# A hybrid FoX/S5 trunk: the mixer's phase doublings moved into pairs 4 to 8 of the first gate and up product, the transposes of c pinned behind their product group

## The chip, the core and the metric

The kernel runs on one core of a Trainium2 chip. The metric is the device time of one execution in microseconds (us), the median of several runs. Engines are named as in the profile: PE is the matrix engine (PEld its weight loads), DVE the vector engine, ACT the scalar engine, POOL the GpSimd engine, SP the engine that issues all DMAs here.

## The reference

Two layers over a sequence of 1024 tokens with 1024 features, all in float32. Layer 0 mixes tokens with forgetting attention, layer 1 with a diagonal complex state-space mixer (S5). Each mixer is followed by a SwiGLU channel mixer of 2816 hidden features, with norms around everything:

```python
for i in range(DEPTH):
    h = rmsnorm(x, mix_pre_gain[i])
    m = fox_mixer(h, ...) if i % 2 == 0 else s5_mixer(h, ...)
    x = x + rmsnorm(m, mix_post_gain[i])
    h = rmsnorm(x, ffn_pre_gain[i])
    x = x + rmsnorm((silu(h @ w_gate[i]) * (h @ w_up[i])) @ w_down[i], ffn_post_gain[i])
```

The S5 mixer needs tables that depend on parameters alone, not on x. From log_dt and lam it forms a = exp(lam dt) (with sine and cosine of the angle), z = (a - 1) / lam, and bb = z * b; it also uses c. These tables are what the change touches.

## The kernel before

The program is recorded in Python, and a list scheduler then places each instruction into its engine's stream by priority; each engine works its own stream strictly in order and waits on semaphores. `keep_in_program_order(op)` holds one instruction back to the place where the program wrote it; without it an instruction may be hoisted or sink. All DMAs stand in one stream, SP's.

**The product of gate and up** (`gate_up`, L830 to L987) works over 11 pairs p = 0 to 10 of 128-row blocks. A pair has 14 product groups s = 0 to 13, each of 12 matmuls (L882; three for each of four k, because every operand is kept as a high and a low part, `ah` and `al`, with `h*h + h*l + l*h`). It is a fast-matrix-product scheme: seven products per m = 0, 1, in the order `A11 B11`, `A12 B21`, `S1 T1`, `S2 T2`, `S3 T3`, `S4 B22`, `A22 T4`, so s = 2 i + m. The products land in PSUM banks X, Y and Z. After each group an eviction copies (ACT, L932, L937, L939) or adds (DVE, L934, L941, L944) the bank into the tiles `s` and `up`, and a bank is written again only when its eviction is done. DVE and ACT also split the next operands: ACT casts the high part (L851), DVE subtracts for the low part (L852), after sums of weight blocks (L864, L865, L870, L871). Weights come by DMA into four `raw` pages (L232), each freed by its last reader. The results go to DRAM (`g_d`, L959 to L967). All streams share PE with this chain of matmuls.

**The tables of the mixer** are a generator, `s5_params`, which `gate_up` advances one step at chosen (p, s) through `next(beside)`; which ones stands in `first` in `trunk`. Its steps, in order: dt and angles; exponentials; sines; powers of a (`powers(pw, 8)`); the phase doublings; z; then bb = z * b (`cmul`, L1211 to L1216) and the four loads of c (L1233); two steps of eight 128x128 PE transposes of c (L1239), each copied out by ACT into `cc` (L1243); then for eight chunks `ch` a chain of POOL products (L1269 to L1273, into `cp`), ACT copies of bb into a block `bs` (L1272), 16 small PE matmuls (L1287), POOL products again (L1330 to L1332, into `bp`), eight PE transposes (L1255), an ACT copy (L1257) and a store `T_d` (L1258). One chunk fills one pair, from pair 3 on. The next chunk's first POOL product writes the page that the store of `T_d` reads.

**The phase doublings** (L1182 to L1193 before) double a table X of angles four times: for n = 1, 2, 4, 8 the entries n+1 to 2n (7 of them at the end) are the first ones plus entry n, brought back into plus or minus pi by six DVE instructions (L1184 to L1189), each on the result of the last. X is read only much later, by `s5_rot` (L1311, after the gate and up product). Their scratch N is the tile `kk` on page 28, which `powers` uses before, and page 28 is also that of `bb`: bb can be written only when the last doubling has read N.

**Pages.** b is loaded on page 34, the scratch of bb's product is on page 32; the two halves of c are loaded into pages 34 and 32 again, so a load of c waits for the last product that reads b or that scratch. The page of R2 holds small tables in columns 512 and up and has its columns 0 to 447 free.

Of the kernel before, what the change touches and what calls it, by code (L numbers as in the profile page):

```python
# [12 lines left out]
ALU = mybir.AluOpType  # L13

P = 128
# [10 lines left out]
MAGIC = 1.5 * 2.0 ** 23  # L26
# [132 lines left out]
class Trunk:  # L159
# [668 lines left out]
    def gate_up(self, B, g_d, beside=iter(()), when=lambda p, s: False):  # L828
# [7 lines left out]
        nc, R = self.nc, self.R  # L836
        V = nc.vector
        n = NF // 2
# [64 lines left out]
        for p, s in order:  # L903
# [22 lines left out]
            m = s % 2  # L926
            a, b, x = steps[s // 2]
            mm(p, m, a, b, bank[x, m], s < 6)
            X, Y, Q = (bank[i, m] for i in "XYZ")
# [52 lines left out]
                prep[s - 10](1)  # L982
            if when(p, s):
                next(beside, None)
        yield

    def down(self, finish, begin=lambda tb, m: None, beside=iter(()), steps=((),) * 3, extra=0, last=3,  # L987
# [89 lines left out]
    def s5_small(self):  # L1077


        nc, A, c, R = self.nc, self.A, self.cst, self.R  # L1080
        V = nc.vector
        tt, ts, stt = V.tensor_tensor, V.tensor_scalar, V.scalar_tensor_tensor
# [17 lines left out]
        ps = self.pb((0, 1), (P, 4, 32))  # L1100
# [26 lines left out]
        ang, n, r = (w[:, 8 + 3 * i:11 + 3 * i] for i in range(3))  # L1127
# [4 lines left out]
        C1 = 6.28125  # L1132
        C2 = math.floor((2 * math.pi - C1) * 2 ** 20) / 2 ** 20
        C3 = 2 * math.pi - C1 - C2
        LIM = 3.141592
# [24 lines left out]
        X = self.ph.rearrange("p i a n -> p n (i a)")  # L1160
# [5 lines left out]
        kk = R("s5t2", (P, 2, 16, 32))  # L1166

        def powers(X, top):
            n = 1
            while n < top:  # L1170
                c_ = min(n, top - n)
                self.cmul(X[:, 0, n + 1:n + 1 + c_], X[:, 1, n + 1:n + 1 + c_], X[:, 0, 1:1 + c_], X[:, 1, 1:1 + c_],
                          X[:, 0, n:n + 1].to_broadcast([P, c_, 32]), X[:, 1, n:n + 1].to_broadcast([P, c_, 32]),
                          kk[:, 0, :c_], kk[:, 1, :c_])
                n += c_

        yield
        powers(pw, 8)
        yield
        n, N = 1, kk.rearrange("p i n a -> p (i n a)").rearrange("p (n m) -> p n m", m=64)  # L1180
        while n < 15:
            c_ = min(n, 15 - n)  # L1182
            x, q = X[:, n + 1:n + 1 + c_], N[:, :c_]
            tt(x, X[:, 1:1 + c_], X[:, n:n + 1].to_broadcast([P, c_, 64]), op=ALU.add)  # L1184
            ts(q, x, 1.0 / (2 * math.pi), MAGIC, op0=ALU.mult, op1=ALU.add)
            V.tensor_scalar_sub(q, q, MAGIC)
            stt(x, q, -C1, x, op0=ALU.mult, op1=ALU.add)
            stt(x, q, C1 - 2 * math.pi, x, op0=ALU.mult, op1=ALU.add)
            ts(x, x, LIM, -LIM, op0=ALU.min, op1=ALU.max)  # L1189
            n += c_  # L1190
            if n == 8:
                yield

        z = self.z = c.tile([P, 2, 32], F32, name="z5")
        u1, u2, u3, nre = tmp(), tmp(), tmp(), tmp()
        ar, ai = Pre[:, 1], Pim[:, 1]
# [21 lines left out]
    def s5_params(self):  # L1218


        nc, A, R = self.nc, self.A, self.R
# [3 lines left out]
        braw, kk = self.braw, R("s5w1", (P, 2, 32, 16))  # L1225
# [4 lines left out]
        craw = [R(f"s5w{i}", (P, 8, 2, HD)) for i in range(2)]  # L1230
# [4 lines left out]
        for i in range(2):  # L1235
            yield
            ps = self.S("psC", (P, 8, P))
            for t in range(8):
                nc.tensor.transpose(ps[:, t], craw[i][:, t].rearrange("p d s -> p (d s)"), self.ident)  # L1239

            for d in range(2):
                r = slice(d * 64, d * 64 + 64)
                nc.scalar.copy(self.cc[r, i].rearrange("p (t a) c -> p t a c", t=8),  # L1243
                               ps[r].rearrange("p t (a b c) -> p t a b c", b=2, c=16)[:, :, :, d])
# [347 lines left out]
def trunk(ctx: ExitStack, tc: tile.TileContext, A, out):  # L1592
    T = Trunk(ctx, tc, A, out)
    nc, R = T.nc, T.R
# [87 lines left out]
    T.fox(hT, og_d, first_norm(range(2, 8), (2, 3, -2, -1)), OUT0)  # L1682
    xr = x0.rearrange("(p b) d -> p b d", b=8)
    R.set(hold=[28, 30, 31, 34, 36, 37], t1=[20], ah=[3, 4, 20], al=[5, 6, 21], er=[29, 32])
    first = {0: (8, 10, 12), 1: (5, 6, 8, 10, 12), 2: (5, 8, 12)}
    B = Operands(T)
    gu = T.gate_up(B, g_d[0], T.s5_params(), lambda p, s: s in first.get(p, (5, 12)))
    end = T.out_proj(lambda tb: xr[:, tb, :], A["mix_post_gain"][0], A["ffn_pre_gain"][0], x1_d, turns, B, lambda: next(gu))
# [130 lines left out]
```

## Time and profile before

| | us |
|---|---|
| median of 3 runs | 2381.59 (2380.56 to 2382.78) |
| the profiled execution | 2379.95 |
| its span | 2378.1 |
| PE busy in the span | 2340.3 (98%) |
| DVE, ACT, POOL busy | 1683.0, 1195.2, 424.1 |

The span runs from the first to the last instruction; 1.85 us of the profiled execution lie outside it. A matmul shows as about 390 ns, but the next one starts some 227 ns behind it: they overlap, so distances are read from starts, not from busy time. In a timeline a row has the start, the duration, the engine, the line, the operation and its tiles, and in brackets the idle time of the engine before it and what ended that. The windows give busy time (and count) of PE, PEld, DVE, ACT and POOL, then the mean clock granted to PE (PEclk), the DMA share and GB/s. Pair 2 of the first gate and up product begins at 811.46 us, pair 4 at about 900, pair 9 at about 1101.

### The profile page before, as it was taken

The numbers are of one execution on the slowest core, as the hardware profiler recorded it, in microseconds if no ns is written. First come the engines' busy times: TensorE is split into PE (matmuls) and PEld (weight loads), VectorE is DVE, ScalarE is ACT, GpSimd is POOL, SyncE is SP. The second block draws the span as 40 slices with busy tenths as digits, with TensorE's granted clock in tenths as the row PEclk, the third lists the DMA queues.
The fourth block names the chain that finished last, engine by engine and source line by source line (L and its number), as shares of the span: only waits on it lengthen the run. The fifth ranks groups of instructions, "written<-read, shape, count | busy, mean of one in ns | idle before, by whom it ended". The sixth has DMA issues, their size and how long they took to land.

```text
span 2378.1 us, 31540 instructions
## 1 busy us (share of the span) xinstructions
PE 2340.3 (98%) x11736; PEld 1942.7 (82%) x11736; DVE 1683.0 (71%) x2684; ACT 1195.2 (50%) x2024; POOL 424.1 (18%) x411
## 2 busy tenths in 40 slices
PE   8999999999999999999999999999999999999998
PEld 6788888888788778888888889888888888888887
DVE  7867787678778966666778686853796656555867
ACT  6766676677745334444554662332463333333443
POOL 3222221222200034545520002410000000000000
PEclk9999999999999999999999999999999999999999
DMA  5121112211433444343598753443434323237874
GB/s 162 37 62 54 54 54 62 63 45 63 139 129 110 120 112 139 118 139 118 184 329 311 268 177 93 148 138 106 131 102 142 111 93 109 91 120 256 289 247 168
DMA packets 256684, 320.61 MB, mean 135 GB/s; under 512 B 34313, under 2 KB 184129, under 8 KB 256530
## 3 DMA queue, kind: packets, MB, share of 16 engines
q1 hardware_dynamic: 256530, 318.59, 41.3%
q8 instruction: 92, 1.51, 0.3%
q14 instruction: 62, 0.51, 0.1%
HBM read 240.82 MB, written 77.72 MB: 134 GB/s over the span
## 4 chain that ended last, share of the span: by engine, by line
PE 80%; DVE 10%; ACT 5%; issue 3%; POOL 1%; DMA 1%; DVEq 0%; SPq 0%; ACTq 0%; POOLq 0%
PE ps L882 32%; PE ps L1003 16%; PE ps L274 7%; PE ps L275 7%; PE ps L276 7%; PE ps L644 2%; PE ps L625 2%; PE ps L586 1%; DVE ps L590 1%; PE ps L587 1%; DVE y L329 1%; DVE ptl L629 1%; ACT y L298 1%; POOL o L652 1%; DMA raw<-in_ffn_w_gate_dram 1%
## 5 line engine op out<-in xcount | busy, mean ns | idle before, releaser
L882 PE MATMUL ps<-B,ah 128*128 128x512 f32 x992 | 306.5, 390 | 0.8 <-DVE B L90 0.6
L1003 PE MATMUL ps<-wdh,gh 128*128 128x512 f32 x616 | 240.0, 390 | 0.6 <-DVE s L924 0.6
L1003 PE MATMUL ps<-wdl,gh 128*128 128x512 f32 x616 | 239.9, 389 | 0.0
L1003 PE MATMUL ps<-wdh,gl 128*128 128x512 f32 x616 | 239.6, 389 | 0.1
L882 PE MATMUL ps<-ops,ah 128*128 128x512 f32 x704 | 220.0, 394 | 1.6 <-ACT s L939 1.6
L882 PEld LDWEIGHTS ps<-B,ah 128*128 128x128 f32 x992 | 186.2, 188 | 40.9 <-DVE B L90 1.2
L274 PE MATMUL ps<-hT,wh 128*128 128x512 f32 x496 | 197.4, 398 | 0.7 <-DVE pt L465 0.2
L276 PE MATMUL ps<-hT,wl 128*128 128x512 f32 x496 | 195.0, 393 | 0.0
L275 PE MATMUL ps<-hT,wh 128*128 128x512 f32 x496 | 194.5, 392 | 0.0
L882 PE MATMUL ps<-B,al 128*128 128x512 f32 x496 | 193.0, 389 | 0.0
L255 ACT CAST gh<-gr 128x1024 fp32r<-128x1024 f32 (+1 forms) x78 | 81.1, 1040 | 163.8 <-PE ps L1003 149.6
L882 PEld LDWEIGHTS ps<-ops,ah 128*128 128x128 f32 x704 | 132.4, 189 | 31.1 <-ACT s L939 2.1
L256 DVE TENSOR_TENSOR gl<-gr,gh 128x1024 fp32r<-128x1024 f32 (+1 forms) x78 | 98.8, 1268 | 79.5 <-ACT gh L255 79.1
L852 DVE TENSOR_TENSOR al<-raw,ah 128x1024 fp32r<-128x1024 f32 x84 | 109.1, 1301 | 55.5 <-ACT ah L851 55.3
L629 DVE TENSOR_TENSOR ptl<-ps,pth 128x512 fp32r<-128x512 f32 x192 | 102.5, 551 | 55.2 <-ACT pth L628 54.3
L1755 POOL TENSOR_TENSOR y<-m,s 128x512 f32<-128x512 f32 x4 | 6.5, 1645 | 750.3 <-DVE m L1030 652.8
L882 PE MATMUL ps<-ops,al 128*128 128x512 f32 x352 | 137.7, 391 | 0.0
L581 POOL TENSOR_TENSOR An<-An,cmask 128x128 f32<-128x128 f32 x128 | 75.4, 591 | 345.8 <-DVE mx L590 321.0
L1003 PEld LDWEIGHTS ps<-wdh,gh 128*128 128x128 f32 x616 | 115.6, 188 | 25.4 <-DVE s L924 1.3
L1003 PEld LDWEIGHTS ps<-wdh,gl 128*128 128x128 f32 x616 | 115.6, 188 | 24.5 <-DVE gl L256 0.5
L1003 PEld LDWEIGHTS ps<-wdl,gh 128*128 128x128 f32 x616 | 115.6, 188 | 23.6
L851 ACT CAST ah<-raw 128x1024 fp32r<-128x1024 f32 x84 | 88.3, 1052 | 90.6 <-PE ps L882 84.4
(393 smaller groups left out, 5886.6 us busy)
## 6 DMA issues: line engine op xcount, KB each, us to landing
raw<-in_ffn_w_down_dram SPq DMA_DIRECT2D x98, 512.0 KB, 5.3
gr<-g_d SPq DMA_DIRECT2D x76, 512.0 KB, 4.5
raw<-in_ffn_w_gate_dram SPq DMA_DIRECT2D x44, 512.0 KB, 4.0
raw<-in_ffn_w_up_dram SPq DMA_DIRECT2D x44, 512.0 KB, 4.5
g_d<-s SPq DMA_DIRECT2D x66, 256.0 KB, 2.0
raw<-in_fox_w_in_dram SPq DMA_DIRECT2D x32, 512.0 KB, 4.3
g_d<-up SPq DMA_DIRECT2D x44, 256.0 KB, 3.1
g_d<-up SPq DMA_DIRECT2D x21, 512.0 KB, 2.7
```

The costliest lines, as they stand in the source:

```text
L255: self.hop = self.hcopy(h, src)
L256: self.lop = self.lsub.tensor_sub(l, src, f32(h))
L274: mm(ps, lh, rh, start=start, stop=False)
L275: mm(ps, lh, rl, start=False, stop=False)
L276: mm(ps, ll, rh, start=False, stop=stop)
L581: nc.gpsimd.tensor_add(An[h][:, qs], An[h][:, qs], self.cmask)
L625: nc.tensor.transpose(p2[:, i], p[:, (g + i) * P:(g + i + 1) * P], self.ident)
L629: nc.vector.tensor_sub(dl, p2[:, 0:n], f32(dh))
L851: nc.scalar.copy(h, src)
L852: V.tensor_sub(l, src, f32(h))
L882: nc.tensor.matmul(bank, x[:, k], y, start=start and k == i == 0, stop=True, skip_group_check=True)
L1003: nc.tensor.matmul(bank, x[:, j, t], y[:, j], start=start and i == 0, stop=True, skip_group_check=True)
```

## The change

- The doublings become a generator of their own, `self.phases`, with their scratch in R2's free columns 0 to 447. `gate_up` advances it once per pair for p > 3, at s = 8. It has five pieces: n = 1 and n = 2 whole in pair 4, the first three instructions of n = 4 in pair 5 and its last three in pair 6, the same of n = 8 in pairs 7 and 8. The first instruction of each piece is pinned.
- `s5_small` has one step fewer, and `first` one entry fewer for pair 1.
- The first transpose of each half of c is pinned to its place in the program, behind the product group (2, 5) or (2, 8).

```diff
@@ gate_up, at the end of each (p, s)
             if when(p, s):
                 next(beside, None)
+            if s == 8 and p > 3:
+                next(self.phases, None)
@@ s5_small
+        pin = self.tc.keep_in_program_order
+
+        def phases():
+            N = R2[:, 0:448].rearrange("p (n m) -> p n m", m=64)
+            for n in (1, 2, 4, 8):
+                c_ = min(n, 15 - n)
+                x, q = X[:, n + 1:n + 1 + c_], N[:, :c_]
+                pin(tt(x, X[:, 1:1 + c_], X[:, n:n + 1].to_broadcast([P, c_, 64]), op=ALU.add))
+                ts(q, x, 1.0 / (2 * math.pi), MAGIC, op0=ALU.mult, op1=ALU.add)
+                V.tensor_scalar_sub(q, q, MAGIC)
+                if n > 2:
+                    yield
+                pin(stt(x, q, -C1, x, op0=ALU.mult, op1=ALU.add))
+                stt(x, q, C1 - 2 * math.pi, x, op0=ALU.mult, op1=ALU.add)
+                ts(x, x, LIM, -LIM, op0=ALU.min, op1=ALU.max)
+                if n > 1:
+                    yield
+
+        self.phases = phases()
         yield
         powers(pw, 8)
         yield
-        n, N = 1, kk.rearrange("p i n a -> p (i n a)").rearrange("p (n m) -> p n m", m=64)
-        while n < 15:
...
-            n += c_
-            if n == 8:
-                yield
@@ s5_params
-                nc.tensor.transpose(ps[:, t], craw[i][:, t].rearrange("p d s -> p (d s)"), self.ident)
+                op = nc.tensor.transpose(ps[:, t], craw[i][:, t].rearrange("p d s -> p (d s)"), self.ident)
+                if not t:
+                    self.tc.keep_in_program_order(op)
@@ trunk
-    first = {0: (8, 10, 12), 1: (5, 6, 8, 10, 12), 2: (5, 8, 12)}
+    first = {0: (8, 10, 12), 1: (5, 6, 8, 10), 2: (5, 8, 12)}
```

The lines of the changed kernel have other numbers: the doublings are L1186 to L1193, bb's product L1218 to L1223, the loads of c L1240, the transposes L1246, the copies of bb L1281.

**DVE, around the product that makes bb.** Before, the last doublings and bb stand among the work of pair 2, groups 2 to 5:

```order
L1187 SCALAR_TENSOR_TENSOR R_775_7458<-s5t_777_7470,R_775_7458 128x7x64
L934 TENSOR_TENSOR up_7690<-up_7690,ps 128x512
L1188 SCALAR_TENSOR_TENSOR R_775_7458<-s5t_777_7470,R_775_7458 128x7x64
L924 TENSOR_TENSOR s_7689<-s_7689,up_7690 128x512
L1189 TENSOR_SCALAR R_775_7458<-R_775_7458 128x7x64
L1213 TENSOR_TENSOR bb_7657<-s5w_790_7655 128x512
L852 TENSOR_TENSOR al_7755<-raw_7423,ah_7754 128x1024
L1214 TENSOR_TENSOR s5w_790_7655<-s5w_774_7455,z_7602 128x512
L1215 TENSOR_TENSOR s5w_790_7655<-s5w_774_7455,z_7602 128x512
L864 TENSOR_TENSOR S_8021<-raw_7840 128x512
L1216 TENSOR_TENSOR bb_7657<-s5w_790_7655 128x512
```

Now bb stands at the end of pair 1 (L957 and L958 are that pair's last sums):

```order
L852 TENSOR_TENSOR al_7589<-raw_7524,ah_7588 128x1024
L1218 TENSOR_TENSOR s5w_787_7592<-s5w_774_7455,z_7546 128x512
L944 TENSOR_TENSOR ez_7056<-up_7406,ps 128x512
L1219 TENSOR_TENSOR s5w_787_7592<-s5w_774_7455,z_7546 128x512
L924 TENSOR_TENSOR s_7055<-s_7055,ez_7056 128x512
L1220 TENSOR_TENSOR bb_7594<-s5w_787_7592 128x512
L957 TENSOR_TENSOR ez_7056<-s_7055,s_7405 128x512
L1221 TENSOR_TENSOR s5w_787_7592<-s5w_774_7455,z_7546 128x512
L1222 TENSOR_TENSOR s5w_787_7592<-s5w_774_7455,z_7546 128x512
L958 TENSOR_TENSOR ez_7056<-s_7055 128x512
L1223 TENSOR_TENSOR bb_7594<-s5w_787_7592 128x512
```

The 24 doubling instructions that stood between are gone from this stretch.

**SP's stream, pairs 1 and 2.** Before, the loads of c stand behind a weight load of pair 2's second half:

```order
L960 DMA g_d<-s_7405 128x512
L961 DMA g_d<-ez_7056 128x1024
L965 DMA g_d<-s_7405 128x512
L966 DMA g_d<-up_7406 128x512
L967 DMA g_d<-up_7406 128x512
L232 DMA raw_7778<-in_ffn_w_gate_dram 128x8x128
L232 DMA raw_7840<-in_ffn_w_up_dram 128x8x128
L959 DMA g_d<-s_7689 128x512
L232 DMA raw_7776<-in_ffn_w_gate_dram 128x8x128
L1233 DMA s5w_792_7664<-in_s_c_re_dram 128x8x64 x2
L1233 DMA s5w_793_7665<-in_s_c_im_dram 128x8x64 x2
L232 DMA raw_7838<-in_ffn_w_up_dram 128x8x128
```

Now they stand ahead of the five stores and three weight loads:

```order
L960 DMA g_d<-s_7405 128x512
L1240 DMA s5w_789_7601<-in_s_c_re_dram 128x8x64 x2
L1240 DMA s5w_790_7602<-in_s_c_im_dram 128x8x64 x2
L961 DMA g_d<-ez_7056 128x1024
L965 DMA g_d<-s_7405 128x512
L966 DMA g_d<-up_7406 128x512
L967 DMA g_d<-up_7406 128x512
L232 DMA raw_7754<-in_ffn_w_gate_dram 128x8x128
L232 DMA raw_7816<-in_ffn_w_up_dram 128x8x128
L959 DMA g_d<-s_7665 128x512
```

On PE the first eight transposes of c stood behind the first matmul of group (2, 8) and the other eight behind its last; now the first eight stand behind the last matmul of group (2, 5), and the other eight where they were.

**DVE in pair 4, behind group 8**, where the first piece of the doublings now stands; the rows of L941, L865, L924 and L944 stood there one behind the other before:

```order
L941 TENSOR_TENSOR s_8323<-s_8323,ps 128x512
L1186 TENSOR_TENSOR R_775_7458<-R_775_7458 128x64
L865 TENSOR_TENSOR S_8607<-S_8607,raw_8415 128x512
L1187 TENSOR_SCALAR R_776_7459<-R_775_7458 128x64
L1188 TENSOR_SCALAR R_776_7459<-R_776_7459 128x64
L1191 SCALAR_TENSOR_TENSOR R_775_7458<-R_776_7459,R_775_7458 128x64
L1192 SCALAR_TENSOR_TENSOR R_775_7458<-R_776_7459,R_775_7458 128x64
L941 TENSOR_TENSOR up_8324<-up_8324,ps 128x512
L1193 TENSOR_SCALAR R_775_7458<-R_775_7458 128x64
L924 TENSOR_TENSOR s_8323<-s_8323,up_8324 128x512
L1186 TENSOR_TENSOR R_775_7458<-R_775_7458 128x2x64
L1187 TENSOR_SCALAR R_776_7459<-R_775_7458 128x128
```

Four more instructions of n = 2 follow before L944. Pairs 5 to 8 have three doubling instructions each at the same place.

More of the change, by code (lines that the diff above doesn't have):

```diff
@@ L1179, in s5_small @@
         yield
-        n, N = 1, kk.rearrange("p i n a -> p (i n a)").rearrange("p (n m) -> p n m", m=64)
-        while n < 15:
[L1182 to L1189, printed above, removed]
-            n += c_
-            if n == 8:
-                yield
         z = self.z = c.tile([P, 2, 32], F32, name="z5")
```

## The prediction

> **What bounds the kernel now.** I read the page first: engine totals and the chain that ended last.
>
> ```profile
> PE 2340.3 (98%) x11736; PEld 1942.7 (82%) x11736; DVE 1683.0 (71%) x2684; ACT 1195.2 (50%) x2024; POOL 424.1 (18%) x411
> PE 80%; DVE 10%; ACT 5%; issue 3%; POOL 1%; DMA 1%; DVEq 0%; SPq 0%; ACTq 0%; POOLq 0%
> ```
>
> PE is the bound. A change that takes no matmul away can only win what PE loses by waiting or by a lower clock, and it moves nothing else unless it makes PE wait anew. So I looked at PE's timeline where the moved work stands, pairs 1 and 2:
>
> ```profile
> 811.46 0.62 PE L882 MATMUL ps<-B,ah 128*128 128x512 f32 x2
> ...
> 825.06 0.61 PE L882 MATMUL ps<-T,ah 128*128 128x512 f32 x2
> 826.95 0.50 PE L882 MATMUL ps<-T,al 128*128 128x512 f32 x1 [1.28 <-DVE al L852]
> ...
> 829.39 0.62 PE L882 MATMUL ps<-ops,ah 128*128 128x512 f32 x2
> ...
> 836.63 0.50 PE L882 MATMUL ps<-ops,ah 128*128 128x512 f32 x1 [1.64 <-ACT s L939]
> 838.65 1.94 PE L1239 MATMUL ps<-ident,s5w 128*128 128x128 f32 x8 [1.51 <-DMA s5w<-in_s_c_re_dram]
> ...
> 844.91 1.03 PE L1239 MATMUL ps<-ident,s5w 128*128 128x128 f32 x8
> 845.71 0.70 PE L882 MATMUL ps<-ops,ah 128*128 128x512 f32 x2
> ```
>
> Five groups of 12 matmuls lie between the first two rows: 13.60 us for 60 starts, 0.2267 us each. Group 5 begins at 825.06 and should take 2.72; group 6 begins at 829.39, so 1.61 us are lost, nearly all of it the wait of 1.28. Groups 6 and 7 need 5.44, so group 8 is due at 834.83, and nothing is lost before (PE falls idle at 836.63 - 1.64 = 834.99, a matmul's overlap later). Group 8 and both sets of transposes need 2.72 + 2 x 0.80 (the second set, 844.91 to 845.71) = 4.32, but group 9 begins only at 845.71: 10.88 us, so 6.56 lost. Only 3.15 of these are the two waits. The rest shows in the windows (sum, then busy time of PE, PEld, DVE, ACT, POOL, then the clock):
>
> ```profile
> 811.40:825.60 14.20, 14.20 (x63) 11.48 (x62) 14.13 (x28) 2.95 (x5) 0.00 (x0) 1.00 0.50 166
> 829.40:834.80 5.40, 5.40 (x25) 4.31 (x23) 5.10 (x8) 1.23 (x5) 0.00 (x0) 1.00 0.39 126
> 834.80:838.60 3.80, 0.70 (x2) 0.19 (x1) 2.46 (x3) 3.19 (x5) 0.00 (x0) 0.91 1.28 239
> 838.60:841.00 2.40, 2.35 (x10) 2.29 (x11) 1.80 (x3) 0.38 (x1) 0.00 (x0) 0.50 1.27 242
> 841.00:845.00 4.00, 4.00 (x12) 3.04 (x11) 0.00 (x0) 0.78 (x2) 0.00 (x0) 0.54 0.20 47
> ```
>
> Behind the pair of waits PE is granted half its clock for 6.4 us, some 3.1 us of work lost though it is "busy". The single wait of 1.28 left the clock at 1.00 in the next window. Together 8.17 us are lost here, 0.34% of the time. The first window shows why: DVE is busy 14.13 of 14.20. What it is late with:
>
> ```profile
> 808.02 0.21 DVE L1185 TENSOR_SCALAR s5t<-R 128x64 f32<-128x64 f32 x1
> 830.27 0.68 DVE L1213 TENSOR_TENSOR bb<-s5w 128x512 f32<-128x512 f32 x1
> 832.61 0.69 DVE L1215 TENSOR_TENSOR s5w<-s5w,z 128x512 f32<-128x512 f32 x1
> 833.81 0.69 DVE L1216 TENSOR_TENSOR bb<-s5w 128x512 f32<-128x512 f32 x1
> 834.53 0.50 ACT L1272 COPY R<-bb 64x64 f32<-64x64 f32 x2 [2.56 <-DVE bb L1216]
> 833.32 1.02 SPq L1233 DMA_DIRECT2D s5w<-in_s_c_re_dram  x2
> ```
>
> One queue explains all three waits. The doublings share DVE with the pair's own work until bb starts at 830.27, and bb needs their scratch page, so L1216 ends at 834.5. ACT stands 2.56 us at the copy of bb, with the cast L851 and L939, the eviction group 8 waits for, behind it. The load of c goes out at 833.32, as L1215 lets page 34 go, and lands 5.3 us later. And the low part `al` of group 5 was itself queued between doublings.
>
> **The change part by part.**
>
> *The doublings leave.* All 24 go, and bb's product starts where the first L1185 stood, 808.02. L1213 to L1216 show 0.60 from start to start (832.61 to 833.81 is two of them). In the new order L1215's counterpart is the ninth instruction from there and L1216's the eleventh: bb is done by about 808.0 + 11 x 0.6 = 814.6, some 20 us earlier. The ACT copy then waits before group 0's eviction, which is not read until group 2; the slip of a few tenths lies under 5 us of matmuls. The load of c is issued at about 813.4 and lands, by the same 5.3, at 818.7, while the transposes now want it at the end of group 5, 827.8: 9 us of cover. The `al` of group 5 loses the doublings ahead of it on DVE, 5 us or more, against 1.28 missing. L939 has no bb copy ahead of it. So I take the whole 8.17 as gone, the clock's part with it, since the waits that preceded the half clock are. From below: if one of the waits stays, see the third rival.
>
> *The loads of c move ahead of five stores and three weight loads* on SP. They can hold it until L1216's counterpart is done, 814.6, and for their own issue, 0.5 us each by the row above. So the stores go out by about 817. They free pages that pair 2 writes again only from its group 4 or 5 on, past 822. Cost 0; uncovered, the delay is at most those 2 to 3 us, once.
>
> *The transposes* are the same 16; the first set moves from inside group 8 to the end of group 5. Cost 0. Their two banks are those of Y, whose products end with group 3, at 811.46 + 48 x 0.2267 = 822.3, 5 us ahead.
>
> *The doublings arrive in pairs 4 to 8*, on a DVE that has idle time there, but not at that place. Their durations (least, median, largest of the four sizes):
>
> ```profile
> L1184 DVE TENSOR_TENSOR R<-R x4: 291/522/966, 793.2 to 822.5; 128x64 f32<-128x64 f32 x1, 128x128 f32<-128x128 f32 x1, 128x256 f32<-128x256 f32 x1, 128x448 f32<-128x448 f32 x1
> L1185 DVE TENSOR_SCALAR s5t<-R x4: 211/325/930, 808.0 to 823.9; 128x64 f32<-128x64 f32 x1, 128x128 f32<-128x128 f32 x1, 128x256 f32<-128x256 f32 x1, 128x448 f32<-128x448 f32 x1
> L1186 DVE TENSOR_SCALAR s5t<-s5t x4: 181/255/396, 808.9 to 825.4; 128x64 f32<-128x64 f32 x1, 128x128 f32<-128x128 f32 x1, 128x256 f32<-128x256 f32 x1, 128x448 f32<-128x448 f32 x1
> L1187 DVE SCALAR_TENSOR_TENSOR R<-s5t,R x4: 264/510/971, 809.6 to 826.8; 128x64 f32<-128x64 f32 x1, 128x128 f32<-128x128 f32 x1, 128x256 f32<-128x256 f32 x1, 128x448 f32<-128x448 f32 x1
> L1188 DVE SCALAR_TENSOR_TENSOR R<-s5t,R x4: 265/496/978, 810.3 to 828.3; 128x64 f32<-128x64 f32 x1, 128x128 f32<-128x128 f32 x1, 128x256 f32<-128x256 f32 x1, 128x448 f32<-128x448 f32 x1
> L1189 DVE TENSOR_SCALAR R<-R x4: 219/347/614, 811.1 to 829.8; 128x64 f32<-128x64 f32 x1, 128x128 f32<-128x128 f32 x1, 128x256 f32<-128x256 f32 x1, 128x448 f32<-128x448 f32 x1
> ```
>
> n = 1 is the sum of the least, 1.43. The median of four is the mean of the middle two, so n = 2 and n = 4 are together 4.91; on a line from 64 to 448 columns n = 2 is 2.0, leaving 2.9. n = 8 is 4.86: 2.29 and 2.56. An instruction with another behind it starts that one 0.09 before its end. Pair 4 thus gets about 3.2 us, pairs 5 to 8 about 1.2, 1.5, 2.0 and 2.3.
>
> What is queued behind them: the evictions of groups 9 to 11 (their banks are wanted 8 us later or more), splits for the next pair, and L958, whose store L961 stands on SP ahead of the store of T_d. For the latter POOL waits, and for POOL's `cp` the small matmuls L1287, in PE's own stream:
>
> ```profile
> 938.30 0.34 SPq L961 DMA_DIRECT2D g_d<-up  x1
> 938.98 0.32 SPq L1258 DMA_DIRECT2D T_d<-s5w  x1
> 942.48 1.10 POOL L1269 TENSOR_TENSOR s5w<-cc,pw 128x512 f32<-128x512 f32 x1 [13.29 <-DMA T_d<-s5w]
> 950.14 3.86 POOL L1273 TENSOR_TENSOR s5w<-s5w 64x512 f32<-64x512 f32 x2
> 956.41 0.83 PE L1287 MATMUL ps<-s5w,R 128*16 128x128 f32 x12
> ```
>
> POOL is done at 954.00, PE comes at 956.41: 2.41 of slack. L961 moves to 941.5, T_d to 941.9, which is 2.9 later, so PE waits 0.5 in pair 5. Pairs 6 to 8 stay under that slack (2.0 at most). Pair 9 has less:
>
> ```profile
> 1112.15 3.86 POOL L1273 TENSOR_TENSOR s5w<-s5w 64x512 f32<-64x512 f32 x2
> 1117.13 1.05 PE L1287 MATMUL ps<-s5w,R 128*16 128x128 f32 x16
> ```
>
> 1.12 of slack against 2.2 of pair 8's piece: 1.1 us. Bounds for the whole new cost: 0, if DVE catches up before L958, and 4.6, if every pair has only pair 9's slack and its piece in full (2.1 + 0.1 + 0.4 + 0.9 + 1.1). I take 1.6.
>
> *Sum.* 8.17 - 1.6 = 6.5 (6.57). The profiled execution's 2379.95 becomes 2373.4. The median of the runs shown lies 1.64 above it: **2375.0 us**.
>
> **The rivals.**
>
> *The chain through T_d costs more in every pair* (the 4.6 above): 8.17 - 4.6 = 3.6, so 2378.0. For it: the slack of 1.12 in pair 9. Against: 2.41 in pair 5, which gets the largest piece.
>
> *A wait stays at group 8.* ACT's new order puts the copies of c and a cast ahead of L939; if that still holds group 8 by the 1.64 + 0.15, at full clock, then 6.5 - 1.8 = 4.7 is won: 2376.9. Against: the copy of bb was what ACT waited at.
>
> *Slower: doublings meet POOL.* In pair 4 the same L870 takes 1.67 beside POOL and 0.69 without:
>
> ```profile
> 925.51 1.67 DVE L870 TENSOR_TENSOR raw<-raw,raw 128x512 f32<-128x512 f32 x1
> 933.31 0.69 DVE L870 TENSOR_TENSOR raw<-raw,raw 128x512 f32<-128x512 f32 x1
> ```
>
> Twelve doubling instructions read two tiles. At 1 us more each, pair 4's six bring its 3.2 to 9.2, and pair 5 waits 9.2 - 0.3 - 2.4 = 6.5. The one, two, one and two of pairs 5 to 8 add waits of 0, 1.1, 0.6 and 3.2, and the longest two waits bring the half clock, 3.1 each: 17.6 in all against 8.17, so 2381.59 + 9.4 = 2391.0. It decides once the new loss passes 8.2. Against it: POOL stands idle 13.29 us up to 942.48, just where the pieces stand. The Trainium skill, "SBUF — State Buffer", section "SBUF: two separate sides", says that a DVE instruction with two inputs from SBUF and a GpSimd instruction that reads SBUF share one port pair as an exclusive lock, the loser blocked for the other's whole length. By that rule the move, out of a stretch where POOL is silent into one where it works, is a risk of just this kind; the row of 1.67 agrees with it, and where it applied the time would be the 2391.0. POOL's idle stretch speaks against its use here.
>
> On the clock's price, the Trainium skill, "TensorE: Matmul & The Clock Gate", section "What's actually happening", has the full clock back after one busy window of about 3.4 us; that would make one half clock cost 1.7 in place of 3.1, an estimate from that page. The windows show 6.4 us at 0.50 to 0.54 here, so the measurement decides.
>
> *Nothing comes of it*, because bb or c are late for another reason: 2381.6.
>
> **How the numbers follow.** Forecast 0.66; T_d in every pair 0.14; a wait at group 8 0.12; slower 0.05; nothing 0.03. What this measurement can tell from no change is 0.2%, 4.8 us: faster means under 2376.8. The forecast lies there (0.66), and half of the third case (0.06): faster 0.72. Same: the rest of that (0.06), the first rival and nothing (0.17): 0.23. Slower 0.05. Range: below, no new wait at all (2381.59 - 8.17 = 2373.4) less the 1.0 by which the fastest run lies under the median: 2372.4. Above, the first rival's 2378.0 and a half for the scatter: 2378.5.
>
> **What would show it.** PE without waits in pair 2, PEclk 1.00 there, ACT's wait at bb gone, group 9 of pair 2 beginning 26.1 us after the pair's first matmul, in place of 34.25. Short PE waits before L1287's counterpart in pairs 5 and 9, ended by POOL. I am wrong if PE still waits for L939 or for c in pair 2, if the new waits in pairs 5 to 9 exceed 3 us, or if PEclk falls in any of them.

## The result and the profile after

| | before | after |
|---|---|---|
| median (us) | 2381.34 (20 runs) | 2386.22 (20 runs) |
| profiled execution (us) | 2379.95 | 2385.12 |
| its span (us) | 2378.1 | 2383.3 |
| PE, DVE, ACT, POOL busy (us) | 2340.3, 1683.0, 1195.2, 424.1 | 2343.1, 1689.6, 1194.3, 425.0 |

The ratio is 1.0018, 95% interval 1.0012 to 1.0024: the kernel became 4.9 us slower, where 6.6 us less were forecast. Engine totals and the chain that ended last, on the page of after:

```profile
PE 2343.1 (98%) x11736; PEld 1944.3 (82%) x11736; DVE 1689.6 (71%) x2684; ACT 1194.3 (50%) x2024; POOL 425.0 (18%) x411
PE 79%; DVE 10%; ACT 4%; issue 3%; POOL 2%; DMA 2%; SPq 0%; DVEq 0%; ACTq 0%; POOLq 0%
```

The totals hardly move. POOL and the DMAs each gain a point of the chain, PE and ACT each lose one.

**Pair 2 did what was forecast.** The stretch 811.40 to 848.60 as one window (sum, then PE, PEld, DVE, ACT, POOL, the clock, DMA share, GB/s), first before, then after, and behind them PE's timeline of after:

```profile
811.40:848.60 37.20, 32.77 (x138) 26.39 (x138) 28.58 (x47) 12.27 (x21) 2.06 (x2) 0.91 0.48 127
```

```profile
811.40:848.60 37.20, 37.20 (x174) 31.00 (x173) 28.64 (x37) 16.00 (x26) 8.14 (x6) 1.00 0.51 134
```

```profile
813.09 0.61 PE L882 MATMUL ps<-B,ah 128*128 128x512 f32 x2
...
829.41 1.03 PE L1246 MATMUL ps<-ident,s5w 128*128 128x128 f32 x8
...
838.47 1.03 PE L1246 MATMUL ps<-ident,s5w 128*128 128x128 f32 x8
...
839.26 0.71 PE L882 MATMUL ps<-ops,ah 128*128 128x512 f32 x2
```

PE is busy throughout, at full clock, and group 9 begins 26.17 us after the pair's first matmul, in place of 34.25: 8.08 us are won.

**The loss is in pairs 5 to 9**, where the pieces now stand. An undisturbed pair takes 40.18 us from one set of T transposes (L1264) to the next. Here are three of these sets in PE's timeline of after, and all its waits over 0.2 us between them:

```profile
929.71 1.03 PE L1264 MATMUL ps<-ident,s5w 128*128 128x128 f32 x8
948.17 0.50 PE L882 MATMUL ps<-T,al 128*128 128x512 f32 x1 [0.64 <-DVE al L852]
952.50 1.05 PE L1296 MATMUL ps<-s5w,R 128*16 128x128 f32 x14 [1.28 <-POOL s5w L1282]
972.70 1.03 PE L1264 MATMUL ps<-ident,s5w 128*128 128x128 f32 x8
...
1031.26 0.50 PE L882 MATMUL ps<-T,al 128*128 128x512 f32 x1 [0.55 <-DVE al L852]
1035.60 1.05 PE L1296 MATMUL ps<-s5w,R 128*16 128x128 f32 x14 [1.28 <-POOL s5w L1282]
...
1076.42 1.05 PE L1296 MATMUL ps<-s5w,R 128*16 128x128 f32 x14 [0.22 <-POOL s5w L1282]
1116.45 0.50 PE L882 MATMUL ps<-T,al 128*128 128x512 f32 x1 [2.00 <-DVE al L852]
1139.49 1.03 PE L1264 MATMUL ps<-ident,s5w 128*128 128x128 f32 x8
```

Pair 5 lasts 972.70 - 929.71 = 42.99, that is 2.81 too long. From 929.71 to 1139.49 there are five pairs, and 209.78 - 5 x 40.18 = 8.88 us are lost. The waits at L1296, on POOL, were forecast in pairs 5 and 9. Those at `al`, on DVE, were not. Added up they are the longer ones (3.2 us against 2.8), but a sum of waits does not say which of them sets the loss. What stands behind pair 5's two waits, on SP, POOL and DVE of after:

```profile
934.72 0.34 SPq L961 DMA_DIRECT2D g_d<-up  x1
935.15 0.38 SPq L1267 DMA_DIRECT2D T_d<-s5w  x1
...
940.63 1.11 POOL L1278 TENSOR_TENSOR s5w<-cc,pw 128x512 f32<-128x512 f32 x1 [18.13 <-DMA T_d<-s5w]
...
944.50 1.56 DVE L864 TENSOR_TENSOR S<-raw 128x512 f32<-128x512 f32 x1 [6.81 <-DMA raw<-in_ffn_w_gate_dram]
...
949.16 3.29 POOL L1282 TENSOR_TENSOR s5w<-s5w 64x512 f32<-64x512 f32 x2
```

T_d goes out 5.44 us after its transposes began, against 2.59 before: 2.85 late, by the forecast's own route (2.9). But POOL begins 5.48 us behind that issue, against 3.50 before. So POOL's chain is 4.8 us late. It ends at 952.45, and the fourteen L1296 matmuls that need its last product begin at 952.50, 22.79 us behind the transposes, where in an undisturbed pair they begin at 20.14. Pair 9 has no wait of over 0.2 us there, only the one of 2.00 at `al`:

```profile
1113.66 0.70 DVE L864 TENSOR_TENSOR S<-raw 128x512 f32<-128x512 f32 x1 [7.79 <-DMA raw<-in_ffn_w_gate_dram]
...
1115.39 3.85 POOL L1282 TENSOR_TENSOR s5w<-s5w 64x512 f32<-64x512 f32 x2
...
1118.94 1.40 PE L1296 MATMUL ps<-s5w,R 128*16 128x128 f32 x16
```

Yet here too the third of the sixteen begins at 1119.29 and POOL ends at 1119.24. In every pair that loses over 0.2 us, in all four profiled executions of this kernel, these matmuls begin 0.04 to 0.06 us behind the end of POOL's chain, whatever PE waited for before. So POOL sets the loss, and the waits at `al` fall into time that PE would have lost at L1296 anyway. Alone they would have cost at most 1.1, 1.0 and 2.3 us in pairs 5, 7 and 9, an estimate: so much later than the undisturbed 20.02 does PE reach its first L1296 matmul. In pair 9 the two paths are thus nearly equal.

The waits at `al` have another origin, the gate load behind the late stores on SP. L864, which reads it, begins 14.8, 14.7 and 17.0 us behind the transposes in these pairs, against 11.4, 11.7 and 12.7 in before. Sharing with POOL can add to that (1.56 us in pair 5 against 0.70 in pair 9), but is nothing new. Pair 5 of before, with POOL on time and no wait:

```profile
947.81 1.27 DVE L864 TENSOR_TENSOR S<-raw 128x512 f32<-128x512 f32 x1 [5.66 <-DMA raw<-in_ffn_w_gate_dram]
```

The chain view of pair 5 of after (929 to 970) names POOL and no DVE:

```profile
by line: PE ps L882 69.3%; POOL s5w L1282 14.2%; POOL s5w L1279 7.7%; POOL s5w L1278 3.5%; PE ps L1296 2.6%; PE ps L1264 2.1%; issue 1.0%
```

In an undisturbed pair that line names PE alone (shown below for the kernel with the pieces at group 3).

Pairs 2 and 5 to 9 together make this execution less than 1 us longer, and its span is longer by 5.2. The rest stands elsewhere: 1.6 us ahead of pair 2, 1.1 at the first group of the down product, 1.6 in the mixer. Run 10's profile loses as much in pairs 5 to 9 and has none of the last two.

### The profile page after: what moved, and what is told of

Read it like the earlier page. It is cut to its first block, busy times and chain, and to the rows that moved or that the text cites. A ratio compares the mean times of both kernels' runs of the same rounds, so it can differ in the third digit from the quotient of the medians.

```text
span 2383.3 us, 31540 instructions
## 1 busy us (share of the span) xinstructions
PE 2343.1 (98%) x11736; PEld 1944.3 (82%) x11736; DVE 1689.6 (71%) x2684; ACT 1194.3 (50%) x2024; POOL 425.0 (18%) x411
## 4 chain that ended last, share of the span: by engine, by line
PE 79%; DVE 10%; ACT 4%; issue 3%; POOL 2%; DMA 2%; SPq 0%; DVEq 0%; ACTq 0%; POOLq 0%
PE ps L882 30%; PE ps L1005 16%; PE ps L274 7%; PE ps L275 7%; PE ps L276 7%; PE ps L644 2%; PE ps L625 2%; PE ps L586 1%; PE ps L587 1%; DVE al L852 1%; DVE ps L590 1%; DVE y L329 1%; DMA raw<-in_ffn_w_gate_dram 1%; DVE ptl L629 1%; ACT y L298 1%
```

## The experiments

The theory, A: pairs 1 and 2 give their 8 us; the pieces at group 8 cost more than that in pairs 5 to 9. The rivals differ in why.

**1. No doublings at all** (left out: the table of angles is filled with zeros, so the doublings' time is gone).

```diff
-            if s == 8 and p > 3:
-                next(self.phases, None)
...
-        V.memset(X[:, 0], 0.0)
+        nc.gpsimd.memset(self.ph, 0.0)
```

> The doublings are left out altogether (the table X is filled with zeros by POOL instead, so the rotation that is read from it is not the right one); all else stands as in the changed kernel. Theory A (pairs 1 and 2 gain 8.2 us, and the doublings' new place in pairs 4 to 8 costs more than that): pair 2 without waits, the steps from one set of L1264's counterpart to the next all 40.2 us, no wait for al or POOL in pairs 5 to 9, and about 8 us less than before, ratio 0.9966. Theory B (the loss comes with the earlier loads of c, bb and the rest of the order, or lies behind the first gate and up product): PE still waits in pairs 5 to 9 or later, and the time is within 3 us of before, ratio 0.999 to 1.001.

Measured 2374.78, ratio 0.9974 (0.9963 to 0.9984). All pairs last 40.18. This is what the change could win: 5.9 us in the medians. So the pieces cost nearly 11 us (4.9 + 5.9), not 1.6.

**2. The pieces at group 0.**

```diff
-            if s == 8 and p > 3:
+            if s == 0 and p > 3:
```

> The same five pieces in the same pairs 4 to 8, but behind group 0 in place of group 8, where DVE has done the last pair's sums and stands 5.5 to 6.6 us waiting for a weight load (L864). Theory A (what costs is the place: DVE has no idle time from group 8 to the end of the pair, and the stores and loads behind it are late): all pieces lie in the idle stretch, no new wait in PE, within 1 us of e1_no_doublings, about 7 to 8 us less than before, ratio 0.997. Theory B (any 10 us of doublings on DVE in these pairs cost about what they take): 2 us or less from the changed kernel, ratio 1.001 to 1.002.

Measured 2377.43, ratio 0.9985 (0.9976 to 0.9994): most of the cost gone, but less than expected. In pair 4 the two pieces run beside POOL, and their tiny instructions swell until `al` is late:

```profile
896.06 0.21 DVE L1187 TENSOR_SCALAR R<-R 128x64 f32<-128x64 f32 x1
...
898.78 1.29 DVE L1193 TENSOR_SCALAR R<-R 128x64 f32<-128x64 f32 x1
...
901.41 1.16 POOL L1278 TENSOR_TENSOR s5w<-cc,pw 128x512 f32<-128x512 f32 x1
901.63 1.07 DVE L1187 TENSOR_SCALAR R<-R 128x128 f32<-128x128 f32 x1
...
909.38 0.50 PE L882 MATMUL ps<-T,al 128*128 128x512 f32 x1 [1.48 <-DVE al L852]
```

That pair loses 1.77 us, a later one 0.72. So sharing with POOL is a cost of its own here, and the place decides how much of it there is.

**3. T_d issued by ACT.**

```diff
-            nc.sync.dma_start(self.T_d[ch], T)
+            nc.scalar.dma_start(self.T_d[ch], T)
```

> The store of T_d is issued from ACT, right behind the copy that fills it, and no longer behind the store L961 in SP's stream; doublings as in the changed kernel. Theory A1 (the chain DVE, L961, T_d, POOL, L1296 makes the larger waits): the waits of L1296's counterpart for POOL go (2.8 us in the trace, and 1 to 2 us lost around them), those for al stay (3.2), so 3 to 5 us less than the changed kernel, ratio to before 0.999 to 1.001. Theory A2 (the weight loads behind the stores set the waits, T_d only shows behind them): the al waits take their place, within 2 us of the changed kernel, ratio 1.001 to 1.002.

Measured 2376.92, ratio 0.9981 (0.9972 to 0.9990): some 9 us under after, more than the 3 to 5 given for the T_d chain. The pieces are still at group 8, and L961 is still late on SP, but T_d no longer stands behind it:

```profile
933.10 0.33 ACTq L1267 DMA_DIRECT2D T_d<-s5w  x1
935.71 0.34 SPq L961 DMA_DIRECT2D g_d<-up  x1
935.97 1.28 POOL L1278 TENSOR_TENSOR s5w<-cc,pw 128x512 f32<-128x512 f32 x1 [12.50 <-DMA T_d<-s5w]
```

Pairs 4 to 9 lose 0.3 us in all; the waits at L1296 and those at `al` are both gone. Two things are mixed in. Without T_d, the order on SP puts a gate load ahead of two stores. And with this store on ACT a kernel loses 1.9 us more than before in the first groups of the down product (2.2 in run 4, 1.8 in run 5; read from the starts of the same matmuls in both traces), so its time understates what it repairs. Runs 4 and 5 take these apart.

**4. T_d by ACT, the gate loads back behind L967.**

```diff
-            self.sp = self.nc.sync.dma_start(raw, src)
+            with self.tc.issue_after(self.behind.ins) if self.behind else nullcontext():
+                self.sp = self.nc.sync.dma_start(raw, src)
...
-                nc.sync.dma_start(g_d[3][p], q1[:, hi])
+                last = nc.sync.dma_start(g_d[3][p], q1[:, hi])
+                self.behind = last if 2 < p < 10 and self.phases else None
```

> T_d issued by ACT, the weight loads of the gate kept behind L967 on SP as in the changed kernel (with T_d on ACT alone they had moved ahead of two stores). If the two waits have two causes, the waits at L1296 (2.8 us in the changed kernel) are gone and those at `al` (3.2 us) stay: about 4 of the 8.9 us left, 2381. If the late store alone makes both, nothing is left, 2377. If the late loads make both, all 8.9 stay, 2386.

Measured 2377.47, ratio 0.9984 (0.9975 to 0.9993): by its time the case "the late store alone makes both". Pair 5 still loses 0.54 us, the others nothing. POOL begins 5.1 to 5.2 us behind the transposes in pairs 5 to 9, a good 1 us earlier than in before, and PE nowhere waits for it. The gate loads go out 10.85, 7.69, 7.65, 8.69 and 9.01 us behind the transposes of pairs 5 to 9, against 9.09, 7.63, 9.55, 8.26 and 10.47 in after. So they are not kept late in pairs 7 and 9, and of the pairs that waited at `al` in after only pair 5 tests a late load without a late store. There L868 (L864 of the other kernels) begins even later than in after, 15.03 us behind the transposes, PE waits 0.20 at `al`, and 0.54 are lost where after loses 2.81. Then, further down, the piece of pair 8 with the instruction inside it (L1196 is L1191, L869 is L865), with POOL's chain early:

```profile
944.01 0.69 DVE L868 TENSOR_TENSOR S<-raw 128x512 f32<-128x512 f32 x1 [4.63 <-DMA raw<-in_ffn_w_gate_dram]
...
1083.63 0.98 DVE L1196 SCALAR_TENSOR_TENSOR R<-R,R 128x448 f32<-128x448 f32 x1
1084.53 0.67 DVE L869 TENSOR_TENSOR S<-S,raw 128x512 f32<-128x512 f32 x1
```

The same piece in after, where POOL is 2.4 us late in pair 8 and still at work there:

```profile
1088.97 3.76 POOL L1341 TENSOR_TENSOR s5w<-s5w,s5w 128x512 f32<-128x512 f32 x2
...
1090.08 1.48 DVE L1191 SCALAR_TENSOR_TENSOR R<-R,R 128x448 f32<-128x448 f32 x1
...
1091.46 1.82 DVE L865 TENSOR_TENSOR S<-S,raw 128x512 f32<-128x512 f32 x1
```

0.98 and 0.67 against 1.48 and 1.82. The pieces of pairs 5 to 8 take 1.30, 1.66, 2.26 and 2.56 us here, 1.82, 2.28, 2.77 and 3.32 in after, and L961 behind them (L965 in this kernel) is later than in before by 1.2, 1.4, 1.4 and 1.2 us here, by 1.8, 3.1, 2.4 and 3.2 in after. So there is a loop: a late T_d makes POOL late, POOL then runs beside the next piece, DVE is late, and with it the next L961, the next T_d and the gate load. How much of it is the piece and how much DVE's late start on the load was not separated.

**5. The kernel before, with T_d by ACT.** The edit of run 3, and nothing of the change.

> The kernel before with the store of T_d issued by ACT instead of SP; nothing of the change. Theory late store (the store and the loads behind it are what the moved doublings made late): before has no wait in pairs 4 to 9, so there is nothing to win; same as before within 2 us, perhaps 1 us slower by a wait at the first group of the down product (1.2 us was seen there in the changed kernel with this store on ACT). Rival, that the store on ACT is a gain of its own whatever the doublings do: 3 us or more faster than before.

Measured 2383.24, ratio 1.0004 (0.9995 to 1.0013): nothing to win in itself, and some loss at the start of the down product, as said.

**6. The pieces in DVE's gap.** On DVE each of the pairs 4 to 8 has a stretch without work, 4.1 to 5.9 us in run 1, between the second `al` of the pair and L865, which waits for a weight load. Recorded at group 3 the pieces stand exactly there; the order on every other engine is that of after.

```diff
-            if s == 8 and p > 3:
+            if s == 3 and p > 3:
```

> The changed kernel with its pieces at group 3 instead of 8, so that on DVE they stand between the second low part `al` and L865, which waits 5.9 us for a weight load there. PE, ACT, POOL and SP keep their order. Theory late store: L961 and T_d keep their early place, so the loss of 8.9 us in pairs 5 to 9 falls under 1 us, and the time is that of the kernel without doublings, about 6 us under before (2375). Rival, that the price is DVE's share or the sharing with POOL, which is busy in that stretch: 3 us or more stay, 2378 or above.

Measured **2373.93, ratio 0.9968 (0.9957 to 0.9979)**: faster than both kernels, by 7.7 us and, against run 10 below, 12.7. All pairs last 40.18. DVE in pair 5, and behind it the chain view from 929 to 970:

```profile
947.59 1.21 DVE L852 TENSOR_TENSOR al<-raw,ah 128x1024 fp32r<-128x1024 f32 x1
948.73 0.58 DVE L1186 TENSOR_TENSOR R<-R 128x256 f32<-128x256 f32 x1
...
952.76 0.75 DVE L865 TENSOR_TENSOR S<-S,raw 128x512 f32<-128x512 f32 x1 [2.71 <-DMA raw<-in_ffn_w_gate_dram]
```

```profile
by line: PE ps L882 94.6%; PE ps L1264 3.5%; PE ps L1296 2.4%
```

The piece only eats idle time: 2.71 us of it are left over. In pair 4, with its twelve instructions, none is left, and PE still does not wait.

**7. The late store alone.** Run 6, with T_d put behind L967 on SP; the pieces stay in the gap, and the gate load goes out early.

```diff
-            nc.sync.dma_start(self.T_d[ch], T)
+            self.td = lambda: nc.sync.dma_start(self.T_d[ch], T)
... (gate_up, s == 13)
-                nc.sync.dma_start(g_d[3][p], q1[:, hi])
+                last = nc.sync.dma_start(g_d[3][p], q1[:, hi])
+                if self.td:
+                    with self.tc.issue_after(last.ins):
+                        self.td()
+                    self.td = None
```

> The kernel with the pieces in the gap at group 3 (2373.9), in which T_d alone is put behind L967 on SP, with a gate load ahead of it: the store is late, the doublings are not in its way, and the loads are early. Theory late store: T_d goes out 6 us or more after the T transposes (2.3 now), POOL starts at 10 us, and PE waits at L1296 for some 1.3 us in each of pairs 4 to 10, with waits at `al` beside them, as POOL's chain meets the splits on DVE: 8 to 14 us slower, about 2385. Rival, that the doublings' own time on DVE was needed for the loss: under 3 us, 2376.

Measured 2415.73, ratio 1.0143 (1.0128 to 1.0159): 41.8 us over run 6, three to five times the 8 to 14 expected. In pair 5 (L1273 is the store of T_d, L1302 the matmuls that wait for POOL), and the row of PE's waits over the whole execution (us in total, times, longest):

```profile
942.32 0.43 SPq L1273 DMA_DIRECT2D T_d<-s5w  x1
...
949.30 1.90 POOL L1284 TENSOR_TENSOR s5w<-cc,pw 128x512 f32<-128x512 f32 x1 [18.57 <-DMA T_d<-s5w]
...
960.66 0.61 PE L1302 MATMUL ps<-s5w,R 128*16 128x128 f32 x2 [4.45 <-POOL s5w L1288]
```

```profile
PE ps L1302 <- POOL s5w L1288: 26.3, 14, 4.5
```

T_d goes out 6.20 us behind the transposes in every pair, against 2.33 to 2.74 in run 6, POOL begins 4.3 to 7.0 us behind that issue, and each of the pairs 4 to 9 loses 5.1 to 8.0 us, with the clock below 1.00 in each of them. The late store suffices, without any doubling in its way: pair 9, which holds no piece, loses 5.9 us. The gate loads go out 3.1 to 3.7 us behind the transposes, and among PE's waits there is none at `al`: a late POOL alone does not make those. The expectation took pair 7 of after as a measure and had no clock in it.

**8. The doublings at their old place**, with the scratch of their own and the pinned transposes of the change.

```diff
-            if s == 8 and p > 3:
-                next(self.phases, None)
...
-        self.phases = phases()
+        pin = lambda op: op
...
         powers(pw, 8)
         yield
+        run(phases())
```

> The doublings back at their old place in the program (after the powers of a), not pinned, but with the scratch in R2 and the transposes of c pinned: bb no longer waits for them, but DVE has their 10 us in pairs 1 and 2 again. Theory A (the page was what held bb, and with bb the copy of bb and the loads of c): the waits of 1.64 and 1.51 and the half clock go (6.6 us), the wait for al of 1.28 stays or doubles, no new waits in pairs 5 to 9: 4 to 6 us less than before, ratio 0.998. Theory B (DVE's fullness in pair 2 was the cause, whatever its order): the waits move to other operands of pair 1 or 2, within 2 us of before, ratio 0.999 to 1.001.

Measured 2377.04, ratio 0.9985 (0.9976 to 0.9994).

**9. The scratch alone.** The kernel before with one expression changed, no pins.

```diff
-        n, N = 1, kk.rearrange("p i n a -> p (i n a)").rearrange("p (n m) -> p n m", m=64)
+        n, N = 1, R2[:, 0:448].rearrange("p (n m) -> p n m", m=64)
```

> The kernel before with one word changed: the doublings' scratch lies in R2 as in the change, all else stays where it was, no pins. If the shared scratch page is what makes bb and c late in pair 2, the waits of 1.64 and 1.51 and the half clock go and a wait at `al` of about 0.5 to 1 stays: 2377, like the changed kernel with its doublings at the old place. If DVE's time is what makes them late, the 8.2 us stay: 2381.5.

Measured 2377.79, ratio 0.9981 (0.9971 to 0.9990): as run 8. What PE still waits for in pair 2, first in run 8, then here:

```profile
825.78 0.50 PE L882 MATMUL ps<-T,al 128*128 128x512 f32 x1 [0.45 <-DVE al L852]
```

```profile
829.22 0.73 PE L882 MATMUL ps<-T,ah 128*128 128x512 f32 x2 [1.32 <-ACT ah L851]
830.49 0.50 PE L882 MATMUL ps<-T,al 128*128 128x512 f32 x1 [0.53 <-DVE al L852]
```

In pair 3 both wait another 1.0 us at `al`. The waits for L939 and for c, and the half clock behind them, go with the scratch page alone. That is about half of the 8 us; moving the doublings out of pair 2 brings the rest, if their new place costs nothing.

**10 to 12. The changed kernel again**, unaltered, once timed and twice for one profile each.

> The changed kernel once more, unaltered. If its loss in pairs 5 to 9 is a property of the order, the starts of the T transposes come again 43.0, 40.2, 42.9, 40.8 and 42.9 us apart (8.9 us over five undisturbed periods of 40.18), whichever way the clock falls in the mixer. If those waits were an accident of one execution, the sum differs by more than 2 us. Time: 1.0018 of before; the extra 1.5 us ahead of the first matmul of the weights and the 0.91 of clock near 1540 us may or may not be there.

> The changed kernel once more, for one profile: its median lies 1 and 5 us above the two executions profiled so far, so something that those two do not show is usual. If it is the clock, a stretch below 1.00 stands behind one of the pairs of waits in pairs 5, 7 and 9, worth about 3 us. If not, PEclk is 1.00 there and the time is somewhere else.

> The same for one more profile: the clock behind the waits of pairs 5, 7 and 9, or another place.

The timed run: 2386.60, ratio 1.0018 (1.0009 to 1.0027). What each of the four profiled executions lost, per pair, over 40.18 us:

| pair | forecast | T_d behind its transposes, before / after | POOL behind them, before / after | lost: after | run 10 | run 11 | run 12 |
|---|---|---|---|---|---|---|---|
| 5 | 0.5 | 2.59 / 5.44 | 6.09 / 10.92 | 2.81 | 2.66 | 5.38 | 5.35 |
| 6 | 0 | 2.61 / 4.40 | 6.28 / 8.09 | 0 | 0 | 0 | 0 |
| 7 | 0 | 2.34 / 5.42 | 6.07 / 10.85 | 2.74 | 2.60 | 5.86 | 5.83 |
| 8 | 0 | 2.65 / 5.04 | 6.33 / 8.71 | 0.64 | 0.60 | 0 | 0 |
| 9 | 1.1 | 3.54 / 6.70 | 7.38 / 11.11 | 2.69 | 2.87 | 7.45 | 3.06 |
| sum | 1.6 | | | 8.88 | 8.73 | 18.69 | 14.24 |

(Differences of the starts of the L1264 sets; the issue and POOL columns are of the profiled executions of before and after.) The mean is 12.6. Less the 8.1 won in pair 2 this is 4.5, near the 4.9 of the medians. Four executions from 8.7 to 18.7 fix such a mean only roughly, and run 11 (2393.39) is slower than all 30 timed ones. Run 11's row of PE's waits, pair 5's two waits in the timeline, and two windows around them:

```profile
PE ps L1296 <- POOL s5w L1282: 10.1, 6, 1.8
```

```profile
950.37 0.39 PE L1296 MATMUL ps<-s5w,R 128*16 128x128 f32 x2 [1.51 <-POOL s5w L1282]
952.58 1.05 PE L1296 MATMUL ps<-s5w,R 128*16 128x128 f32 x14 [1.81 <-POOL s5w L1282]
```

```profile
949.00:953.00 4.00, 0.81 (x10) 0.52 (x12) 2.40 (x2) 0.49 (x1) 3.45 (x2) 1.00 0.00 0
953.00:957.50 4.50, 4.50 (x20) 3.44 (x17) 0.00 (x0) 2.13 (x6) 2.12 (x2) 0.62 0.91 288
```

Here the first wait is not at `al` but at L1296 too, so the two stand 2.2 us apart, PE works 0.81 of 4.00 us, and the clock falls to 0.62 for 4.5 us, a loss of 0.38 x 4.5 = 1.7. In after they stand 4.3 us apart and the clock stays at 1.00. Both executions have POOL at the same distance (10.92 and 10.98), but in run 11 L864 begins 0.3 us earlier (14.46 against 14.79) and takes 0.69: which of the two happens is decided by tenths.

## Why the prediction was wrong

- **"I take the whole 8.17 as gone"**: right. In the traces pair 2 has neither the waits nor the half clock, and run 6, where the pieces cost nothing elsewhere, measures 7.7 us.
- **"The doublings leave" as the reason**: half right. Run 9 shows that the shared scratch page made bb and c late, which the prediction did name; the doublings' time on DVE is the other half. Of the whole change, one expression brings 4.3 us.
- **"L961 moves to 941.5, T_d to 941.9, 2.9 later"**: right, 2.85.
- **"PE waits 0.5 in pair 5"**: the step that failed. The path was right (L961, T_d, POOL, L1296); its sizes were not. The step let POOL start as late as T_d goes out, that is, it kept the landing at 3.5 us. Where T_d goes out 5.4 us or more behind its transposes POOL began 4.4 to 5.5 us behind it in after; where it goes out at 5.04 or earlier, 3.7. So POOL was late by 4.8, twice the slack of 2.41, and pair 5 lost 2.81.
- **"Pairs 6 to 8 stay under that slack"**: wrong for pair 7, and by a little for pair 8. The forecast set T_d's delay equal to the piece. T_d was late by 1.8, 3.1, 2.4 and 3.2 us in pairs 6 to 9, against pieces of 1.2, 1.5, 2.0 and 2.3, by the loop that run 4 shows and the forecast had no term for.
- **The sum with measured sizes.** POOL's delays of 4.83, 1.81, 4.78, 2.38 and 3.73 us in pairs 5 to 9, each less the forecast's own slack (2.41, in pair 9 1.12), give 7.4 of the 8.9 us. T_d's delays alone would give 3.2, the later landing adds the other 4.2. What remains, 1.5, was not taken apart.
- **The gate load behind the late stores** had no term either. It makes the waits at `al`. Here POOL's lateness covers them; a late load alone cost 0.5 in pair 5 (run 4), and no run kept it late alone in pairs 7 and 9.
- **The rival "doublings meet POOL"** looked at the moved instructions alone, at 1 us each in pair 4, and was put down by POOL's idle stretch up to 942.48. That stretch holds for pair 4; it does not once POOL is late, as the pieces of pairs 5 to 8 show, 0.5 to 0.8 us each.
- **The upper bound of 4.6** was built of slack and pieces alone and so could not hold 8.9, still less the mean of 12.6. With that in place of 1.6 the sum is 8.17 - 12.6 = -4.4. The part of it that is the clock, at 0.62 in run 11, had no term.
- **"I am wrong if the new waits in pairs 5 to 9 exceed 3 us"** was the right sign to name: PE's waits there came to 6.0 us in after.
- The range ended at 2378.5. The case "slower" got its chance from a price of 17.6 at the extreme, and its threshold, a new loss over 8.2, was passed, but by another road than the one that it priced.

## What to carry to other kernels

Before work is moved onto an engine "with idle time", find the idle stretch itself in the timeline, behind which instruction and ahead of which wait it lies, and put the work there: the same 24 instructions cost 12.7 us more at group 8 than at group 3. Price a move by the first transfer that stands behind it in a queue and whatever waits for that transfer, on other engines too, and treat a slack as a cliff: below it nothing, above it the wait, the neighbours it then collides with, and the clock. Do not read a loss off a sum of waits: 3.2 us at `al` lay inside the time that POOL cost. When a shared scratch page makes something late, give it its own first; that one expression was half of the gain, and moved nothing.

## What the runs showed that was not expected

**One-input instructions swell beside POOL as well.** In run 2 L1187 on 128x128 took 1.07 us beside POOL's L1278 (1.16); in after, with POOL idle, 0.27, and L1193 on 128x64 took 0.22 against 1.29:

```profile
925.06 0.22 DVE L1193 TENSOR_SCALAR R<-R 128x64 f32<-128x64 f32 x1
...
926.28 0.27 DVE L1187 TENSOR_SCALAR R<-R 128x128 f32<-128x128 f32 x1
```

The prediction exposed only the twelve instructions that read two tiles. The Trainium skill, "SBUF — State Buffer", section "SBUF: two separate sides", gives the exclusive lock to a DVE instruction with two SBUF inputs or in a 2-port mode; the 2-port mode is what the prediction passed over. The rows agree with a lock, as the short instruction takes about as long as POOL's; whether these ran in such a mode, no run here shows.

**The clock's price is not one number.** The half clock in pair 2 of before lasted 6.4 us by the windows and cost 3.1; the one in pair 5 of run 11 cost 1.7. By the records of the granted clock in all these traces a stretch of half clock between 800 and 1600 us lasts either 3.41 or 6.83 us; in pair 2, which run 5 leaves as it was, it was 6.83 in before and 3.41 in run 5. The Trainium skill, "TensorE: Matmul & The Clock Gate", section "What's actually happening", has the full clock back after at least one busy window of about 3.4 us, by which the least price is 1.7, an estimate from that page: run 11's pair 5 agrees with one window, before with two. Another such stretch (0.91 of the clock over 20 us, 1.8 us) stands in the mixer near 1540 in some executions and not in others, of the changed kernel and of several others alike.

**A 512 KB store landed 3.3 to 6.9 us behind its issue on SP**, with nothing of its own changed but when it was issued and what stood around it there. Why it lands later when it goes out late was not settled. In pair 5 of run 7, where the landing was longest, smaller stores and a gate load had gone out shortly ahead of it and another weight load went out 0.5 us behind it; in pair 6 of after it landed in 3.56 us with the stores as close behind it as in pair 5, where POOL began 5.48 us behind it.
